# The adaptive-norm vector of a diffusion block: weight blocks as the stationary operand of TensorE, and value and key projections a quarter at a time

## The chip, the cores and the metric

The kernel runs as one program on one core of a Trainium2 chip. The metric is the device time of one execution in microseconds (us); the comparison is by the median of several executions. Engine names are those of the profile: PE is TensorE (PEld its weight loads), DVE is VectorE, ACT is ScalarE, POOL is GpSimd, SP is SyncE, which only issues DMA here.

## The reference

One transformer layer for 512 latent tokens of width 1024 with 256 context tokens. What matters here is how a conditioning vector enters: its SiLU is multiplied by a 1024 x 6144 matrix, and the six thirds of the product shift, scale and gate the layer. `mod_c` is the same for the context's vector, of which only the first two parts are used.

```python
mod_x = (silu(c) @ w_ada + b_ada)          # 1024 -> 6 x 1024
mod_c = silu(c_ctx) @ w_ada + b_ada
sh1x, sc1x, g1x, sh2x, sc2x, g2x = split(mod_x, 6)
hx = rmsnorm(x, norm1_g) * (1 + sc1x) + sh1x
hc = rmsnorm(ctx, norm1_g) * (1 + sc1c) + sh1c
q, k, v, u, ga, gp = split(hx @ w_in + b_in)       # k and v also of hc
x = x + g1x * ((sigmoid(ga) * (attn(q, k, v) @ wa) + sigmoid(gp) * (pool(u) @ wp)) @ w_out)
h2 = rmsnorm(x, norm2_g) * (1 + sc2x) + sh2x
x = x + g2x * moe(h2)                              # top 4 of 32 experts
return rmsnorm(x, final_g)
```

All is fp32. The kernel keeps that accuracy by splitting operands into a high part and a residual and adding three products (`mm3`).

## The kernel before

Activations lie channel-major: channel tile k (128 of 1024) on the partitions, tokens along the free axis. The work is written out by hand in the order in which each engine is to do it (`tc.manual_schedule`); every engine takes its instructions in that order.

**Start.** `x_load` brings the tokens, `norm1` scales them, `ht(k)` transposes channel tile k of all 768 tokens into a PSUM buffer (tag S, two of them). `wada` chunks of 1024 x 256 (1 MB) arrive in four pairs j, scale part (1) and shift part (0); each pair serves channel tiles 2j and 2j+1. `ada_mm` multiplies a chunk on TensorE with the conditioning vectors `sil` as the stationary operand (128 x 2) and the chunk as the moving one, 256 columns; the 2-row result is copied (`ada_row1`) and turned into columns by small transposes (`ada_t`). For j = 1 to 3 the scale chunk is multiplied on VectorE (latent vector) and GpSimd (context vector) instead: `gemv`, whose partial sums over the partitions come from matmuls with ones (L288). `ada_t` ends with the columns `mod` and `sca`; `h1(k)` then applies them on ScalarE and splits the result into `hx` and `hc` on VectorE. `v_part(j)` adds two channel tiles to the value projection. Of the first key tile, channel tiles 0 to 5 come before the last `v_part`; the rest of K (`k_mm`) and the first two Q tiles follow.

**Attention stage.** 16 units of 4 heads x 128 queries, each cut into six slices k. Into each slice a few matmuls of a stream (Q of later groups and the two gates, `fps`, L710) are put, by the tables `FPW` and `UW`. One more `w_ada` chunk per unit is worked on, ten in all (`ada_at`): VectorE multiplies half of its columns (`ada_mul_d`, L636 and L638, spread over the slices by `ADN`), GpSimd the other (`ada_mul_p`), and a unit later two matmuls with ones sum over the partitions (`ada_sum`, L643).

**Branch stage.** Sixteen projection tiles (L972), in whose loop the last six chunks are multiplied (`ada_mul`) and summed to rows (`ada_out`, L466). Then follow the output projection, the router, and 32 experts, whose weights stream in.

Of the kernel before, what the change touches and what calls it, by code (L numbers as in the profile page):

```python
# [43 lines left out]
R_C, R_CC, R_N1, R_PS, R_BIN, R_BADA, R_END = 0, 8, 16, 24, 32, 68, 108  # L44
# [24 lines left out]
def body(ctx, tc, x, c, cx, c_ctx, w_ada, b_ada, norm1_g, norm2_g, w_in, b_in, attn_sink, w_pool,  # L69
# [180 lines left out]
    def gemv(j):  # L250
        raw = wad.pop((j, 1))
        g = [wk.tile([P, 256], F32, tag=t, bufs=3, name="gem") for t in ("ph", "pl")]
        for k in range(KT):
            o = g[k % 2]
            if k < 2:
                dve.tensor_scalar(o, raw[:, k, :], sil[:, k, 0:1], None, op0=ALU.mult)
            else:
                dve.scalar_tensor_tensor(o, raw[:, k, :], sil[:, k, 0:1], o, op0=ALU.mult, op1=ALU.add)
        pr = [hw([P, 4, 256], F32, "gemp") for i in range(2)]
        for i in range(2):  # L260
            ks = slice(4 * i, 4 * i + 4)
            pool.tensor_mul(pr[i], raw[:, ks, :], sil[:, ks, 1:2].to_broadcast([P, 4, 256]))
        pool.tensor_add(pr[0], pr[0], pr[1])
        pool.tensor_add(pr[0][:, 0:2], pr[0][:, 0:2], pr[0][:, 2:4])
        pool.tensor_add(pr[0][:, 0], pr[0][:, 0], pr[0][:, 1])
        dve.tensor_add(g[0], g[0], g[1])
        gem[j] = (g[0], pr[0][:, 0, :])

    def ada_mm(j):
        pm = adt[j] = ps_b("PJ", "ada")  # L270
        for part in (1, 0) if j == 0 else (0,):
            raw = wad.pop((j, part))
            for k in range(KT):
# [3 lines left out]
    def ada_row1(j):  # L277
        n = L if j == 0 else 256
        mrow = wb([2, L], F32, "mrow")
        act.copy(mrow[:, 0:n], adt[j][0:2, 0:n])  # L280
        adt[j] = mrow

    def ada_t(j):
        mrow, pt, k0 = adt.pop(j), hts[2 * j], 2 * j
        for q in range(4):
            if j and q > 1:
                for v in range(2):
                    pe.matmul(pt[:, 768 + 2 * q + v:769 + 2 * q + v], gem[j][v][:, (q - 2) * P:(q - 1) * P],  # L288
                              onesf[:, 0:1], start=True, stop=True)
            else:  # L290
                pe.transpose(pt[:, 768 + 2 * q:770 + 2 * q], mrow[:, q * P:(q + 1) * P], ident[0:2, 0:2])
        for part in (1, 0):
            r = part * KT + k0
            dve.tensor_add(mod[:, r:r + 2, :],
                           pt[:, 768 + 4 * part:772 + 4 * part].rearrange("p (m s) -> p m s", s=2),
                           col[:, R_BADA + r:R_BADA + r + 2, None].to_broadcast([P, 2, 2]))
# [3 lines left out]

    gem = {}
    adt = {}
# [38 lines left out]

    with tc.manual_schedule():
        x_load(0)
        vec = wb([R_END, P], F32, "vec")
        for r, ap in ((R_C, c[0]), (R_CC, c_ctx), (R_BADA, b_ada[0, 0:5120]), (R_N1, norm1_g[0]),
# [13 lines left out]
        nc.sync.dma_start(rope, rope_t)  # L359
        norm1(0)  # L360
# [9 lines left out]
        ht(0)  # L370
        ht(1)
        for i in range(4):
            k = slice(2 * i, 2 * i + 2)
            split(wvh[:, k], wvl[:, k], wvr[:, k])
        ada_mm(0)
        ada_row1(0)
        gemv(1)
        for j in range(4):
# [70 lines left out]
    def ada_mul(raw):  # L449
# [6 lines left out]
        for k in range(1, KT):  # L456
            dve.scalar_tensor_tensor(a0, raw[:, k, 0:P], sil[:, k, 0:1], a0, op0=ALU.mult, op1=ALU.add)
            if k % 2:
                yield
# [1289 lines left out]
```

## Time and profile before

| | us |
|---|---|
| median of 3 executions (1839.09 to 1844.54) | 1843.96 |
| profiled execution, its own time | 1846.71 |
| its span, first to last instruction | 1844.9 |
| TensorE busy | 1730.0 |
| VectorE busy | 1616.3 |
| ScalarE busy | 1121.6 |
| GpSimd busy | 442.6 |

The mean granted TensorE clock of the profiled execution is 0.968 of full speed (2.4 GHz); where it is throttled it stands at 0.50 (1.2 GHz). In the rows, times are from the span's start; "PE L1020 MATMUL lcps<-wr,acol 128*128 128x32" is a matmul at line 1020 with a stationary block of 128 x 128 and a moving one of 128 rows and 32 columns. An fp32 matmul shows as two records, an fp32r one as one.

### The profile page before, as it was taken

What the parts mean: (1) busy time and instruction counts of PE and PEld (TensorE: products, weight loads), DVE (VectorE), ACT (ScalarE), POOL (GpSimd) and SP (SyncE); (2) the same over time, 40 slices, a digit from 0 to 9 for tenths busy, and PEclk for the clock granted to TensorE, in tenths of its full rate; (3) what the DMA queues carried; (4) which work ended last, traced back from release to release, by engine and by line L of the source; (5) the groups of instructions that cost most, each with busy time, mean ns of one, the idle gap of its engine ahead of it and who ended that gap; (6) DMA issues with size and microseconds to landing.
All of it is one profiled execution on the core that took longest, in us unless ns stands there. A gap on an engine that the chain in (4) does not pass through costs nothing. (4 is left out here: it accounts for less than half of the span.)

```text
span 1844.9 us, 22641 instructions
## 1 busy us (share of the span) xinstructions
PE 1730.0 (94%) x8380; PEld 1281.8 (69%) x8380; DVE 1616.3 (88%) x1687; ACT 1121.6 (61%) x1194; POOL 442.6 (24%) x275
## 2 busy tenths in 40 slices
PE   4997989999999989999999999999999999999994
PEld 2676767777778857777666777777777777777763
DVE  6469998866786689998999999999999999999994
ACT  3155656763333256777576777667777777776762
POOL 5035453412341011415241211111121121112001
PEclk8799999999999989999999999999999999999997
DMA  9031422233575599999899999999999999999972
GB/s 329 3 115 52 132 80 81 98 110 110 183 237 181 192 305 323 368 369 378 314 376 357 367 366 372 367 360 374 377 364 366 378 363 367 379 362 365 376 278 100
DMA packets 180238, 506.00 MB, mean 274 GB/s; under 512 B 12491, under 2 KB 68952, under 8 KB 180124
## 3 DMA queue, kind: packets, MB, share of 16 engines
q1 hardware_dynamic: 172028, 484.04, 72.2%
q0 software_dynamic: 8096, 20.48, 4.3%
q8 instruction: 67, 1.10, 0.2%
q14 instruction: 47, 0.39, 0.1%
HBM read 489.89 MB, written 22.69 MB: 278 GB/s over the span
## 5 line engine op out<-in xcount | busy, mean ns | idle before, releaser
L1553 DVE TENSOR_TENSOR mwl<-mw,mwh 128x2048 fp32r<-128x2048 f32 x384 | 873.2, 2283 | 37.7 <-PE gu L1283 28.0
L1546 ACT CAST mwh<-mw 128x2048 fp32r<-128x2048 f32 x384 | 727.1, 1910 | 256.2 <-PE dn L1283 116.6
L1283 PE MATMUL gu<-mwh,xT 128*96 128x512 f32 x2048 | 522.2, 397 | 3.0 <-DVE xT L125 2.7
L1283 PEld LDWEIGHTS gu<-mwh,xT 128*96 128x96 f32 x2048 | 326.5, 162 | 139.6 <-DVE xT L125 3.1
L1288 POOL DMA_INDIRECT acc<-y,igs x31 | 119.2, 3845 | 912.8 <-DVE y L1396 912.8
L1283 PE MATMUL gu<-mwl,xT 128*96 128x512 f32 x1024 | 280.5, 396 | 3.0 <-DVE mwl L1553 3.0
L1283 PE MATMUL dn<-mwh,aT 128*96 128x512 f32 x992 | 253.1, 397 | 0.0
L1283 PEld LDWEIGHTS gu<-mwl,xT 128*96 128x96 f32 x1024 | 165.9, 162 | 76.1 <-DVE mwl L1553 3.5
L1283 PEld LDWEIGHTS dn<-mwh,aT 128*96 128x96 f32 x992 | 155.4, 162 | 61.3
L1283 PE MATMUL dn<-mwl,aT 128*96 128x512 f32 x496 | 134.8, 393 | 0.0
L710 PE MATMUL fps<-hx,whi 128*128 128x512 f32 x352 | 122.8, 407 | 1.8 <-ACT rope_t L594 0.8
L1283 PEld LDWEIGHTS dn<-mwl,aT 128*96 128x96 f32 x496 | 79.9, 161 | 34.7
L1244 POOL DMA_INDIRECT xgb<-h2d,igs x31 | 87.0, 2805 | 39.7 <-DVE ltok L1178 16.9
L1373 ACT ACTIVATE gs<-gs 96x1024 f32<-96x1024 f32 x32 | 34.0, 1062 | 90.2 <-DVE gs L1370 90.2
L710 PEld LDWEIGHTS fps<-hx,whi 128*128 128x128 f32 x352 | 66.9, 191 | 18.0 <-ACT gzt L583 2.3
L710 PE MATMUL fps<-hx,wlo 128*128 128x512 f32 x176 | 70.8, 402 | 2.0 <-POOL wlo L695 2.0
L514 ACT ACTIVATE prob<-S,nm 128x512 f32<-128x512 f32 (+1 forms) x64 | 47.8, 747 | 35.4 <-DVE nm L510 34.7
L521 PE MATMUL tp<-ident,prob 128*128 128x128 f32 x288 | 45.6, 282 | 14.5 <-DVE pl L529 14.5
L529 DVE TENSOR_TENSOR pl<-tp,ph 128x512 fp32r<-128x512 f32 x72 | 49.2, 684 | 9.5 <-ACT ph L525 9.0
L509 DVE TENSOR_REDUCE nm<-S 128x1 f32<-128x512 f32 (+1 forms) x64 | 47.9, 749 | 6.4 <-PE S L484 6.0
L1396 DVE SCALAR_TENSOR_TENSOR y<-dn,gts,g2r 96x512 f32<-96x512 f32 x64 | 44.9, 740 | 4.9 <-PE dn L1283 4.9
L525 ACT CAST ph<-tp 128x512 fp32r<-128x512 f32 x72 | 42.0, 584 | 5.2 <-PE tp L521 4.6
(405 smaller groups left out, 2587.7 us busy)
## 6 DMA issues: line engine op xcount, KB each, us to landing
mw<-in_w_gu_dram SPq DMA_DIRECT2D x256, 1024.0 KB
mw<-in_w_down_dram SPq DMA_DIRECT2D x128, 1024.0 KB
wada<-in_w_ada_dram SPq DMA_DIRECT2D x24, 1024.0 KB
gz<-gzt SPq DMA_DIRECT2D x16, 256.0 KB
sg<-gz SPq DMA_DIRECT2D x16, 256.0 KB
wo<-in_w_out_dram SPq DMA_DIRECT2D x4, 1024.0 KB
xt<-in_x_dram SPq DMA_DIRECT2D x2, 1024.0 KB
xh<-in_x_dram SPq DMA_DIRECT2D x4, 512.0 KB
```

What stands on the lines that cost most here:

```text
L509: dve.reduce_max(nmh, S[:, 0:W], axis=AX.X)
L514: act.activation(U["prob"][:, h, 0:W], S[:, 0:W], AF.Exp, bias=nmh, scale=SCALE, accum_out=U["den"][:, h:h + 1])
L521: pe.transpose(U["tp", j][:, h * P:(h + 1) * P], U["prob"][:, h, j * P:(j + 1) * P], ident)
L525: act.copy(U["ph", j], U["tp", j])
L529: dve.tensor_sub(pl, U["tp", j], U["ph", j].bitcast(F32))
L710: pe.matmul(pt, a[:, k, :], b(k), start=n == 0, stop=n == 3 * KT - 1)
L1244: pool.indirect_dma_start(out=xg, out_offset=None, in_=h2d, in_offset=bass.IndirectOffsetOnAxis(ap=ig, axis=0), bounds_check=L - 1, oob_is ...
L1283: pe.matmul(os_[j], lhs(a, k), b[:, k, j * L:(j + 1) * L], start=first and j not in seen, stop=last and j not in left)
L1288: pool.indirect_dma_start(out=acc, out_offset=bass.IndirectOffsetOnAxis(ap=iscat, axis=0), in_=y, in_offset=None, bounds_check=L - 1, oob_ ...
L1396: dve.scalar_tensor_tensor(st["y"][:, cs], st["dn"][n], st["gt"], g2r[0:CAP, cs], op0=ALU.mult, op1=ALU.mult)
L1546: act.copy(hi, raw)
L1553: eng.tensor_sub(lo, raw, hi.bitcast(F32))
```

## The change

All of `w_ada` is now multiplied on TensorE, with 128 x 128 blocks of the chunk as the stationary operand and `sil` as the moving one: two columns in the start, one later. The result is a column per channel at once, so that the row copies, the transposes, `gemv`, `ada_mul`, `ada_mul_p`, `ada_mul_d` and `ada_out` are gone, as is the table `ADN`. In the attention stage thirteen chunks are done instead of ten, one at the end of each unit 0 to 12; three are left to the branch stage. The start goes quarter by quarter: transposes, the quarter's two chunks, `h1`, the quarter of V; the first key tile now gets channel tiles 0 to 3, 4 and 5, and 6 and 7 behind the second, third and fourth quarter, in an S buffer of PSUM, so that from the third quarter on only one of those is left for transposes.

```diff
+    def ada_cols(o, raw, v):
+        for m in range(2):
+            for k in range(KT):
+                pe.matmul(o(m), raw[:, k, m * P:(m + 1) * P], v(k), start=k == 0, stop=k == KT - 1)
     def ada_mm(j):
-        pm = adt[j] = ps_b("PJ", "ada")
-        for part in (1, 0) if j == 0 else (0,):
-            raw = wad.pop((j, part))
-            for k in range(KT):
-                pe.matmul(pm[0:2, part * 256:part * 256 + 256], sil[:, k, :], raw[:, k, :], start=k == 0,
-                          stop=k == KT - 1)
...
+        pm = ps_b("PJ", "ada")[:, 0:8].rearrange("p (a m s) -> p a m s", a=2, m=2)
+        for part in (1, 0):
+            ada_cols(lambda m: pm[:, part, m], wad.pop((j, part)), lambda k: sil[:, k, :])
...
+    def k_part(m, ks):
+        wh, wl = kw[m]
+        if m not in kps:
+            kps[m] = ps_s("kps")
+        for o, h0, h1 in ((kps[m][:, 0:L], hxa(0), hxa(1)),
+                          (kps[m][:, L:L + LC], lambda k: hc[0][:, k, :], lambda k: hc[1][:, k, :])):
+            for k in ks:
+                pe.matmul(o, wh(k), h0(k), start=k == 0, stop=False)
+                pe.matmul(o, wl(k), h0(k), start=False, stop=False)
+                pe.matmul(o, wh(k), h1(k), start=False, stop=k == KT - 1)
...
         wada_load(1)
+        wkr = load_w(w_in[:, OK:OK + 256], "wk_")
         wada_load(2)
-        wkr = load_w(w_in[:, OK:OK + 256], "wk_")
         wada_load(3)
...
+            ht(2 * j)
             if j < 2:
-                gemv(j + 2)
+                ht(2 * j + 1)
+            ada_mm(j)
+            h1(2 * j)
+            if j >= 2:
+                ht(2 * j + 1)
+            h1(2 * j + 1)
+            if j == 0:
+                for i in range(4):
+                    k = slice(2 * i, 2 * i + 2)
+                    split(wvh[:, k], wvl[:, k], wvr[:, k])
+            v_part(j)
+            if j == 1:
+                kw[0] = halves(wkr, 0)
+                k_part(0, range(4))
             if j == 2:
-                kw0 = halves(wkr, 0)
-            if j == 3:
-                kx = ps_b("PJ", "kps")
-                mm3(kx, *kw0, hxa(0), hxa(1), 6, last=False)
-            v_part(j)
-        kw = [kw0, halves(wkr, 1)]
+                k_part(0, range(4, 6))
+                kw[1] = halves(wkr, 1)
         for t in range(NT + NTC):
             v_out(t)
+        k_part(0, range(6, 8))
...
     def ada_sum(raw):
         pt = ps_b("PT", "adaps")
-        for m in range(2):
-            pe.matmul(pt[:, m:m + 1], raw[:, 0, m * P:(m + 1) * P], onesf[:, 0:1], start=True, stop=True)
+        ada_cols(lambda m: pt[:, m:m + 1], raw, lambda k: sil[:, k, 0:1])
         return pt
...
-    NADA = 10
-    ada_at = {u: u for u in range(8)}
-    ada_at[9], ada_at[11] = 8, 9
+    NADA = 13
...
-                q = ada_at.get(u - 1)
-                if k == 5 and q is not None:
-                    aps = ada_sum(araw[q])
+                q = u if k == 5 and u < NADA else None
+                if q is not None:
+                    aps = ada_sum(araw.pop(q))
...
-            if i % 2 == 0:
-                for _ in ada_mul(adas[q]):
-                    pass
-            else:
-                ada_out(q, adas.pop(q))
-                if q + 2 < 16:
-                    adas[q + 2] = ada_load(q + 2, 2 + q % 2)
+        if i % 2 and q < 16:
+            ada_col(q, ada_sum(adas.pop(q)))
+            if q + 2 < 16:
+                adas[q + 2] = ada_load(q + 2, 2 + q % 2)
+            if q == 15:
+                ada_row_out(12, 16)
```

How the order moves, at three places. TensorE in the start, from the first transposes to the first value matmuls (`hT` is the transposed input, `ada` the vector's PSUM tile, `vps` the value accumulator). Before:

```order
L307 MATMUL hT<-ident,xt_107 128x128 x2
L274 MATMUL ada<-wada,sil 2x256 x16
L291 MATMUL hT<-ident,mrow 128x2 x4
L274 MATMUL ada<-wada,sil 2x256 x8
L307 MATMUL hT<-ident,xt_105 128x128 x2
```

and with the change:

```order
L271 MATMUL hT<-ident,xt_107 128x128 x2
L253 MATMUL ada<-sil,wada 128x2 x32
L292 MATMUL vps<-bv,onesf 128x256
L296 MATMUL vps<-wvh,hx_77 128x256
L297 MATMUL vps<-wvh,hx_79 128x256
```

The second pair's matmuls and the next transposes no longer stand between the first pair and the value part: 32 matmuls of two columns, then directly V, which needs `hx`.

VectorE in the same place (`gem` is the partial product of `gemv`, `wvl` the residual of the value weights). Before:

```order
L125 TENSOR_TENSOR wvl<-wv__128,wvh 128x512 x4
L256 TENSOR_SCALAR gem<-wada,sil 128x256 x2
L258 SCALAR_TENSOR_TENSOR gem<-wada,sil,gem 128x256 x6
L266 TENSOR_TENSOR gem<-gem 128x256
L294 TENSOR_TENSOR mod<-hT,col 128x4 x2
L297 SCALAR_TENSOR_TENSOR sca<-mod,col 128x4
L313 CAST hx_77<-th 128x512
```

and with the change:

```order
L262 TENSOR_TENSOR mod<-ada,col 128x4 x2
L264 SCALAR_TENSOR_TENSOR sca<-mod,col 128x4
L277 CAST hx_77<-th 128x512
L278 TENSOR_TENSOR hx_79<-th,hx_77 128x512
L281 CAST hc_81<-tcx 128x256
L282 TENSOR_TENSOR hc_82<-tcx,hc_81 128x256
L277 CAST hx_77<-th 128x512
L278 TENSOR_TENSOR hx_79<-th,hx_77 128x512
L281 CAST hc_81<-tcx 128x256
L282 TENSOR_TENSOR hc_82<-tcx,hc_81 128x256
L125 TENSOR_TENSOR wvl<-wv__128,wvh 128x512 x4
```

`mod` comes first now, and the value weights are split behind the first quarter's `h1`.

TensorE at the end of a unit of the attention stage (`pv` is the unit's output, `fps` the stream, `adaps` the vector's columns). Before:

```order
L537 MATMUL pv<-ph,vx 128x512
L538 MATMUL pv<-pl,vx 128x512
L643 MATMUL adaps<-onesf,wada_668 128x1 x2
L710 MATMUL fps<-hx_77,whi 128x512
L710 MATMUL fps<-hx_77,wlo 128x512
```

and with the change:

```order
L478 MATMUL pv<-ph,vx 128x512
L479 MATMUL pv<-pl,vx 128x512
L253 MATMUL adaps<-sil,wada_702 128x1 x16
L635 MATMUL fps<-hx_78,whi 128x512
L635 MATMUL fps<-hx_78,wlo 128x512
```

Sixteen one-column matmuls stand where two stood; the stream follows as before.

## Rows read from the trace of the kernel before

**Rows 1.** The page, TensorE's granted clock in 40 slices, tenths of full speed.

```profile
PEclk8799999999999989999999999999999999999997
```

**Rows 2.** Busy time by stage: stretch; PE, PEld, DVE, ACT, POOL; clock, DMA share, GB/s.

```profile
32.00:72.20 40.20, 25.81 (x80) 16.92 (x81) 25.45 (x34) 4.95 (x9) 18.27 (x12) 0.53 0.35 115
...
72.20:123.60 51.40, 51.14 (x321) 43.29 (x319) 30.58 (x66) 21.19 (x38) 5.39 (x3) 1.00 0.26 82
...
123.60:354.50 230.90, 198.53 (x1097) 162.36 (x1098) 210.15 (x400) 149.68 (x334) 121.01 (x95) 0.97 0.27 87
...
468.00:571.00 103.00, 97.75 (x409) 75.92 (x407) 82.31 (x108) 35.87 (x47) 43.67 (x32) 0.97 0.63 200
...
655.00:1844.90 1189.90, 1156.26 (x5283) 813.05 (x5282) 1121.50 (x760) 807.39 (x559) 210.37 (x66) 0.98 0.96 349
```

**Rows 3.** The same of two units of the attention stage: units 1 and 14.

```profile
144.10:167.00 22.90, 15.73 (x86) 12.83 (x85) 22.32 (x32) 11.40 (x26) 17.14 (x13) 0.93 0.15 47
...
368.70:382.00 13.30, 13.30 (x87) 11.68 (x86) 10.48 (x22) 10.36 (x23) 2.59 (x2) 1.00 0.30 101
```

**Rows 4.** Waits of TensorE, 123.6 to 354.5 us: total, times, longest.

```profile
PE tp L521 <- DVE pl L529: 14.5, 10, 4.3
```

**Rows 5.** Timeline (start, us, instruction): loads for one-column matmuls, half and full clock.

```profile
66.54 0.50 PEld L288 LDWEIGHTS hT<-onesf,gem 128*128 128x128 f32 x2
...
67.78 0.55 PEld L288 LDWEIGHTS hT<-onesf,gemp 128*128 128x128 f32 x2
...
90.25 0.30 PEld L288 LDWEIGHTS hT<-onesf,gem 128*128 128x128 f32 x2
...
90.92 0.30 PEld L288 LDWEIGHTS hT<-onesf,gemp 128*128 128x128 f32 x2
```

**Rows 6.** Narrow matmuls in the timeline, and the busy time of stretches about them.

```profile
571.20 1.97 PE L1020 MATMUL lcps<-wr,acol 128*128 128x32 f32 x16 [0.71 <-DMA wr<-in_w_router_dram]
...
573.90:577.30 3.40, 3.40 (x19) 3.40 (x18) 3.31 (x5) 0.62 (x1) 0.00 (x0) 0.50 1.01 353
...
640.68 3.71 PE L1198 MATMUL x<-oh,xh 128*128 128x96 f32 x16
...
640.70:644.40 3.70, 3.70 (x21) 3.68 (x21) 2.03 (x7) 0.85 (x1) 0.00 (x0) 0.50 1.01 383
```

**Rows 7.** Timeline of TensorE in the start.

```profile
18.62 1.06 PE L307 MATMUL hT<-ident,xt 128*128 128x128 f32 x4
...
42.58 2.82 PE L307 MATMUL hT<-ident,xt 128*128 128x128 f32 x12 [10.62 <-ACT tcx L316]
...
52.61 1.22 PE L328 MATMUL vps<-bv,onesf 1*128 1x256 f32 x2
...
65.90 0.41 PE L334 MATMUL vps<-wvl,hc 128*128 128x256 f32 x1
```

**Rows 8.** Timeline of VectorE in the start: weight split, `mod`, `h1`.

```profile
22.05 2.50 DVE L125 TENSOR_TENSOR wvl<-wv__128,wvh 128x512 fp32r<-128x512 f32 x4 [3.52 <-ACT wvh L120]
...
68.45 0.23 DVE L294 TENSOR_TENSOR mod<-hT,col 128x4 f32<-128x4 f32 x2 [12.60 <-PE hT L288]
...
71.92 0.69 DVE L314 TENSOR_TENSOR hx<-th,hx 128x512 fp32r<-128x512 f32 x1
...
72.85 0.42 DVE L318 TENSOR_TENSOR hc<-tcx,hc 128x256 fp32r<-128x256 f32 x1
```

**Rows 9.** Timeline of TensorE: K part of six channel tiles, then V.

```profile
91.17 0.48 PE L131 MATMUL kps<-hx,whi 128*128 128x512 f32 x1
...
95.35 0.28 PE L332 MATMUL vps<-wvh,hx 128*128 128x256 f32 x1
...
95.47 0.28 PE L333 MATMUL vps<-wvh,hx 128*128 128x256 f32 x1
```

**Rows 10.** Branch stage: a wait of TensorE, and the busy time behind it.

```profile
PE adaps L466 <- issue: 4.1, 1, 4.1
...
485.00:492.10 7.10, 6.09 (x14) 4.25 (x15) 3.77 (x6) 2.73 (x4) 0.00 (x0) 0.52 0.42 135
```

More of the change, by code (lines that the diff above doesn't have):

```diff
@@ L283, in ada_t @@
[L283 to L291, printed above, removed]
+    def ada_cols(o, raw, v):
+        for m in range(2):
+            for k in range(KT):
+                pe.matmul(o(m), raw[:, k, m * P:(m + 1) * P], v(k), start=k == 0, stop=k == KT - 1)
@@ L292, in ada_t @@
+    def ada_mm(j):
+        pm = ps_b("PJ", "ada")[:, 0:8].rearrange("p (a m s) -> p a m s", a=2, m=2)
+        for part in (1, 0):
+            ada_cols(lambda m: pm[:, part, m], wad.pop((j, part)), lambda k: sil[:, k, :])
+        k0 = 2 * j
         for part in (1, 0):
             r = part * KT + k0
-            dve.tensor_add(mod[:, r:r + 2, :],
-                           pt[:, 768 + 4 * part:772 + 4 * part].rearrange("p (m s) -> p m s", s=2),
+            dve.tensor_add(mod[:, r:r + 2, :], pm[:, part],
@@ L344, in body @@
         vec = wb([R_END, P], F32, "vec")
-        for r, ap in ((R_C, c[0]), (R_CC, c_ctx), (R_BADA, b_ada[0, 0:5120]), (R_N1, norm1_g[0]),
+        for r, ap in ((R_C, c[0]), (R_CC, c_ctx), (R_BADA, b_ada[0]), (R_N1, norm1_g[0]),
                       (R_PS, pool_scale[0]), (R_BIN, b_in[0])):
@@ L447, in ada_load @@
         return raw
-    def ada_mul(raw):
-        r1 = raw[:, :, P:]
-        pool.tensor_mul(r1, r1, sil[:, :, 0:1].to_broadcast([P, KT, P]))
-        for h in (4, 2, 1):
-            pool.tensor_add(r1[:, 0:h, :], r1[:, 0:h, :], r1[:, h:2 * h, :])
-        a0 = raw[:, 0, 0:P]
-        dve.tensor_scalar(a0, a0, sil[:, 0, 0:1], None, op0=ALU.mult)
[L456 to L459, printed above, removed]
-    def ada_out(q, raw):
-        part, cc = divmod(q, 4)
-        o = wb([1, 256], F32, "adab")
-        nc.sync.dma_start(o, b_ada[0:1, 2 * D + q * 256:2 * D + (q + 1) * 256])
-        pt = ps_b("PT", "adaps")
-        pe.matmul(pt[0:1, 0:256], onesf[:, 0:1], raw[:, 0, :], start=True, stop=True)
-        dve.tensor_add(o, o, pt[0:1, 0:256])
-        nc.sync.dma_start(adad[part:part + 1, cc * 256:(cc + 1) * 256], o)
     def att_scores(S, qs, g, n, h, lo_b, nl):
@@ L563, in body @@
     pool.memset(zr, 0.0)
-    acol = cp.tile([P, 24], F32, name="acol")
+    acol = cp.tile([P, 32], F32, name="acol")
     post, lazy, due, cnt = [], [], [], [0]
@@ L737, in body @@
         aps = None
[L738 to L740 removed]
+        kput0 = k_epi(0, kps[0][:, 0:L], kps[0])
+        k_part(1, range(KT))
         wq0 = halves(wqr, 0)
@@ L805, in body @@
                     due.remove(d)
-                if k == 5 and q is not None:
+                if q is not None:
                     ada_col(q, aps)
-                if k == 5 and u == 13:
-                    ada_row_out()
-                if k == 0 and q is not None:
-                    for kk in ADN[k]:
-                        ada_mul_d(araw[q], kk)
-                q = ada_at.get(u)
-                if k and q is not None:
-                    if k == 3:
-                        ada_mul_p(araw[q])
-                    for kk in ADN[k]:
-                        ada_mul_d(araw[q], kk)
+                if k == 5 and u == NADA:
+                    ada_row_out(0, 12)
                 wsum += FPW[k] * UW.get(u, 1.0)
@@ L956, in body @@
     raw, braw, sgs = None, br_load(0), br_gate(0)
-    adas = {NADA: ada_load(NADA, 2), NADA + 1: ada_load(NADA + 1, 3)}
-    for dst, part in ((g1b, 2), (t2b, 3)):
+    adas = {NADA + i: ada_load(NADA + i, 2 + (NADA + i) % 2) for i in range(2)}
+    for dst, part in ((g1b, 2), (t2b, 3), (s2b, 4)):
         nc.sync.dma_start(dst, bc_row(adad[part - 2], D))
```

90 lines of the change are left out of this document (11 added, 79 removed).

## The prediction, on record before the changed kernel was run

> **What bounds the kernel now.** I read the summary's clock line first, then the busy time by stage, then inside the stages that the change touches: the waits, the timeline, and the granted clock of short stretches.
>
> The clock line [rows 1] shows full speed nearly everywhere, with its loss in the first slices. By stages [rows 2]: the start falls into two halves. From 32.0 to 72.2 us TensorE is busy for 25.8 of 40.2 us, at a mean clock of 0.53. It waits 10.6 us for `h1`, which waits for the modulation vector [rows 7], and then works at half speed. From 72.2 to 123.6 us, where the first score matmul starts, it is busy for 51.1 of 51.4 us at full clock. The attention stage up to 354.5 us (the thirteen units 0 to 12) takes 230.9 us: TensorE is busy for 198.5, VectorE for 210.2. So it waits for VectorE in some units; the longest in sum are for the residual of the probabilities, 14.5 us [rows 4]. In a unit without modulation work, such as 368.7 to 382.0 us, TensorE has no gap at all, against 15.7 of 22.9 us in unit 1 [rows 3]. From 655 us on, nothing is changed; TensorE is busy for 1156 of 1190 us there [rows 2], and its weight loads have a fixed ring of buffers, so I let every microsecond of the first 655 pass through to the end.
>
> **The price of the new block.** The change multiplies one 1024 x 256 chunk by 16 fp32 matmuls with a 128 x 128 stationary block and one or two moving columns. The nearest rows are the sums over partitions (L288), the same stationary shape with one moving column. At half clock three of them take from 66.54 to 67.78 us, 0.413 us each; at full clock 90.25 to 90.92, 0.223 us each [rows 5]. A chunk then costs 3.6 us at full and 6.6 us at half clock; the two chunks of one step of the start, 7.1 or 13.2 us.
>
> Which of the two? Eight fp32 matmuls of 32 columns (L1020, two records each) keep TensorE busy for 2 us from 571.2 us; right behind them the clock is at 0.50 from 573.9 to 577.3 us, though the dense output projection has begun. Eight of 96 columns (L1198) keep it busy for all of 3.7 us from 640.7 us and end at 0.50 as they began [rows 6]. So being busy with narrow matmuls neither holds the clock nor brings it back, and one or two columns are narrower than any of these. I take the blocks as losing the clock. The Trainium skill ("TensorE: Matmul & The Clock Gate", section "Why this matters for your kernels") says that the clock is lost through idle gaps between bursts of matmuls; a block has no gap, and by that rule alone the sum would be that of the first rival below, 1849 us. The rows just named speak against reading it so.
>
> **The start.** Removed: three chunks' multiplications on VectorE and GpSimd (`gemv`), the row copies and transposes (`ada_row1`, `ada_t`). Added: eight chunks instead of five on TensorE, and TensorE now runs each quarter as a chain: block, `mod`, `h1`, V part. I follow it.
>
> - Block 0 starts at 19.7 us behind the first transposes, as now; four of those take 1.06 us, half clock [rows 7]. 13.2 us: 32.9.
> - `mod` to the second channel tile's last residual takes 4.2 us (68.45 to 72.61), 4.9 with the context's [rows 8]; the first split of the value weights, now behind it, 0.6 more: 38.4.
> - V part 0 runs at half clock now: five of its six token tiles take from 52.61 to 66.3 us [rows 7]. 13.7, and 1.5 for the rest of the first: 53.6.
> - Twelve transposes 2.8 [rows 7], block 1 13.2, chain 4.2: 73.8. Up to here it is level with now (75.0 us).
> - V part 1 has 36 matmuls of 0.12 us, K part 0 to 3 twelve of 0.232 (18 take from 91.17 to 95.35) and twelve of 0.12 [rows 9]: 8.5. A dense run behind a narrow one begins at half clock. The spell at 573.9 us, within dense work, lasts 3.4 us [rows 6] and so costs 1.7: 84.0.
> - Quarters 2 and 3: six transposes 0.7; a block, between 7.1 and 13.2 since the clock is up when it starts, 10.2 taken (the middle, for want of a nearer row); the chain, now 5 because the K accumulator holds one of the two PSUM buffers and the second tile's transposes come behind the first tile's `h1`; V and K part 6.4 and 1.7. Quarter 2 ends at 108.0; 123.9 for the chain of quarter 3.
> - Then dense: V 4.3, K rest 2.1, second K tile 8.5, Q 48 x 0.232 = 11.1, a spell 1.7: 151.6; first score at 152.
>
> That is **28 us later** than 123.6. Low end: blocks 2 and 3 at full clock and no spells, 11 less, +17. High end: both at half clock and their dense runs too, 15 more, +43. The queue of loads on SyncE is no bound: `wk` goes ahead of two chunks and the last chunk waits for the buffer of block 1's first half, free near 63 us, and is wanted at 114. That cover is 50 us.
>
> **The attention stage.** Ten chunks' multiplications go from VectorE and GpSimd, thirteen blocks come to TensorE. TensorE's work in units 0 to 12 now is 198.5 busy less 6.9 (lost to spells of half clock: the stage's mean is 0.97 of 230.9 us [rows 2]; in unit 1 it is 0.93 [rows 3]) less 4.5 (ten pairs of the old sums at 0.223): 187.1 at full clock. The blocks add 13 x 16 x 0.223 = 46.4. Each block is followed by dense stream matmuls, and I charge one spell of 1.7 per block: 22. Some waiting stays, above all in the first units, which are filled with rotary work; I leave 5 of the 32.4 us that TensorE idles in this stage. Sum 261 against 230.9: **30 us longer**. Low end +18 (half of the blocks without a spell), high end +40 (some with two). VectorE's load falls below TensorE's, so its lateness no longer counts. The pending `ada_col` makes VectorE wait for the block; behind it stands the next unit's maximum, which needs scores that TensorE issues after the block anyway.
>
> **The branch stage.** Removed: the wait of 4.1 us for the first product and the half clock behind it, 7.1 us at 0.52, 3.4 lost [rows 10]; six one-row sums of two pairs' time, 0.45 each, 2.7. Added: three blocks with a spell each, 15.9. **+6 us** (+1 to +10). Rows of the bias and the outputs, now two DMAs instead of seven, and the broadcast of the scale row moved ahead of the loop are not waited for: the stage's only long wait is the one named. GpSimd is far from any bound.
>
> **Sum.** 28 + 30 + 6 = 64. The profiled execution took 1846.7 us, 2.7 above the runs' median of 1844.0; on the median the forecast is 1908.
>
> **Rivals.**
> 1. The blocks keep the clock. Then block 0 ends at 26.8, V part 0 takes 7.6, and so on with full prices: first score at about 120, -4; attention 187.1 + 46.4 + 5 = 239, +8; branch +1. 1849. For it: TensorE has no gaps in a block. Against: [rows 6]. Chance 0.13.
> 2. Faster: the start gains more than the rest loses. What it would take: the half-clock stretch from 32.0 to 72.2, 14.4 us idle and 25.8 at half speed [rows 2], becomes one dense run. 14.4 and 12.9 go, the three added chunks cost 10.7, the chains hide under V and K parts: -16. With attention +3 and branch +1, 1832. It decides if the clock is up from block 0 on. In attention nothing can be gained: TensorE has 32.4 idle, 6.9 and 4.5, together 43.8 us to give back, 3.4 per block, and a block costs 3.6 even at full clock. Chance 0.05.
> 3. The clock stays low for longer than one spell behind every block, in the start as well: attention +22 more, start +43, branch +10. 1949. For it: from 640.7 the clock stays at half through all the narrow work [rows 6]. Against: the dense stream behind a block is long. Chance 0.10.
>
> The forecast has 0.72.
>
> **How the numbers follow.** A measurement can tell about 0.3% (5.5 us) from no change. Forecast and rival 3 are slower (0.82), and of rival 1, which lies near that edge, 0.04: 0.86. Within: 0.08 of rival 1. Faster: rival 2 and 0.01 of rival 1: 0.06. The sum's own ends (each stage's low or high end together) are 1844 + 36 = 1880 and 1844 + 93 = 1937. To hold 8 in 10, I go from 1868 (part of the way to rival 1) to 1945 (nearly all the way to rival 3). What is left out is rivals 1 and 2, 0.18, and little else.
>
> **What would show it.** Right: granted clock about half in every block of two-column matmuls and just behind it; first score near 152 us; 0.41 us a matmul in blocks 0 and 1; units 0 to 12 at 18 to 21 us each, without waits for VectorE; VectorE less busy than TensorE in every unit; the branch stage without its 4 us wait. Wrong: a clock of 1.0 through the blocks with first scores before 125 us; blocks much cheaper than 0.22 us a matmul; or TensorE still idle in the units for VectorE.

## The result and the profile after

The changed kernel takes 1910.9 us (median of 4 executions, 1904.6 to 1917.2), the kernel before 1842.1 beside it: 1.037 times as long, with a 95% interval of 1.033 to 1.042. The forecast was 1908, between 1868 and 1945. The profiled execution took 1904.6 us, the shortest of the four, 6.3 below the median; the stages are read from it, so they say nothing of these 6.3. The page of it, span, busy time of each engine and the clock line that answers to [rows 1]:

```profile
span 1902.6 us, 23561 instructions
PE 1821.8 (96%) x8983; PEld 1395.7 (73%) x8983; DVE 1495.7 (79%) x1532; ACT 1120.4 (59%) x1191; POOL 340.4 (18%) x196
...
PEclk9778989899999989999999999999999999999997
```

TensorE is busy for 92 us more than before, VectorE for 121 less. The clock line has lost tenths in slices 3, 4, 6 and 8: what the line showed lost only at the very start before is now lost in the attention stage too. (Its first slice has gained one; the last section says why that is no gain.) Busy time by stage, the same columns as [rows 2], but with the changed kernel's own borders (first score at 150.3 us, unit 13 at 408.2, branch from 522.1 to 629.9, experts from 715.4):

```profile
72.20:150.30 78.10, 71.82 (x396) 66.42 (x395) 25.33 (x54) 19.73 (x35) 5.39 (x3) 0.76 0.16 54
150.30:408.20 257.90, 251.44 (x1474) 219.13 (x1474) 152.35 (x323) 149.72 (x335) 74.70 (x55) 0.90 0.28 94
522.10:629.90 107.80, 107.25 (x494) 89.65 (x492) 49.59 (x56) 37.18 (x48) 9.87 (x7) 0.94 0.52 165
715.40:1902.60 1187.20, 1153.71 (x5281) 811.45 (x5280) 1121.09 (x759) 807.50 (x559) 213.31 (x66) 0.99 0.96 350
```

The two profiled spans differ by 57.7 us, the two medians by 68.9. The start has 26.7 of them (first score at 150.3 instead of 123.6), units 0 to 12 have 27.0 (257.9 instead of 230.9), the branch stage 4.7 (107.9 instead of 103.2, up to the router's first matmul). The rest is level: the stretches between, 199.4 instead of 197.5, and the experts, 1187.2 instead of 1189.7.

In the attention stage TensorE is now the bound by far: 251.4 of 257.9 us, VectorE 152.4. Its waits there, the two longest; the first of them is one wait in unit 0, and what stood in [rows 4], 14.5 us for the residual `pl`, is nearly gone. The third line is a stretch that begins within the block of unit 4 (247.2 to 251.9 us): TensorE has no gap in it, and the clock is at half.

```profile
PE S L413 <- ACT prob L455: 3.2, 1, 3.2
PE pv L479 <- DVE pl L470: 1.7, 3, 1.0
...
249.40:256.20 6.80, 6.80 (x27) 6.03 (x27) 0.90 (x3) 0.40 (x1) 0.00 (x0) 0.50 0.89 300
```

And the start on TensorE's timeline (start, duration, line): the four blocks, what stands behind the second and the third, and the first score; the last line is busy time and clock from 4 us into the third block to near the end of its V part.

```profile
19.58 13.65 PE L253 MATMUL ada<-sil,wada 128*128 128x2 f32 x64
...
53.40 2.20 PE L271 MATMUL hT<-ident,xt 128*128 128x128 f32 x12
55.43 11.05 PE L253 MATMUL ada<-sil,wada 128*128 128x2 f32 x64
68.26 0.58 PE L296 MATMUL vps<-wvh,hx 128*128 128x256 f32 x1 [1.77 <-DVE hx L277]
...
81.51 9.93 PE L253 MATMUL ada<-sil,wada 128*128 128x2 f32 x64
93.24 1.54 PE L271 MATMUL hT<-ident,xt 128*128 128x128 f32 x6 [1.80 <-ACT tcx L280]
...
106.11 10.56 PE L253 MATMUL ada<-sil,wada 128*128 128x2 f32 x64
...
150.27 0.39 PE L413 MATMUL S<-kkc,qs 128*128 128x256 f32 x1 [1.03 <-DVE qs L401]
...
85.60:102.70 17.10, 14.40 (x65) 13.73 (x66) 4.99 (x12) 3.40 (x5) 0.00 (x0) 0.50 0.18 57
```

A block of 32 narrow matmuls takes 13.65 us where the clock is at half (0.43 each) and 10 to 11 where it is up at its beginning and falls within it. The gaps between a block and the V part behind it are short, 1.8 us and in the last two quarters 0.75 more.

### The profile page after: what moved, and what is told of

The parts are those of the page before. It is cut to its first block, busy times and chain, and to the rows that moved or that the text cites. A ratio compares the mean times of both kernels' runs of the same rounds, so it can differ in the third digit from the quotient of the medians.

```text
span 1902.6 us, 23561 instructions
## 1 busy us (share of the span) xinstructions
PE 1821.8 (96%) x8983; PEld 1395.7 (73%) x8983; DVE 1495.7 (79%) x1532; ACT 1120.4 (59%) x1191; POOL 340.4 (18%) x196
## 5 line engine op out<-in xcount | busy, mean ns | idle before, releaser
L635 PE MATMUL fps<-hx,whi 128*128 128x512 f32 x352 | 130.9, 432 | 1.4 <-ACT rope_t L535 0.8
L635 PEld LDWEIGHTS fps<-hx,whi 128*128 128x128 f32 x352 | 71.4, 205 | 17.9 <-ACT gzt L524 1.7
L253 PEld LDWEIGHTS adaps<-sil,wada 128*128 128x128 f32 x512 | 64.7, 205 | 1.2
L253 PE MATMUL adaps<-sil,wada 128*128 128x1 f32 x512 | 63.1, 257 | 0.0
L276 ACT ACTIVATE th<-hT,mod,sca 128x512 f32<-128x512 f32 x8 | 6.2, 777 | 94.0 <-DVE sca L264 61.8
```

The costliest lines, as they stand in the source:

```text
L253: pe.matmul(o(m), raw[:, k, m * P:(m + 1) * P], v(k), start=k == 0, stop=k == KT - 1)
L276: act.activation(th, pt[:, 0:L], AF.Identity, bias=mod[:, k, 0:1], scale=sca[:, k, 0:1])
L635: pe.matmul(pt, a[:, k, :], b(k), start=n == 0, stop=n == 3 * KT - 1)
```

## The experiments

**Theory.** A block of narrow matmuls costs TensorE its own time and, besides, the clock: dense work behind it runs at half for a while. **Rivals.** Only TensorE's own work counts, and the clock is an accident of the stage. Or, in the start: the serial order of the quarters costs, not the clock. "Lost to half clock" below is a stretch times one less its mean clock; the clock stands in the rows with two digits, so for the attention stage such a figure is good to some 1.3 us.

**1. The chunk as the moving operand, in nine of thirteen units and in the branch.**

```diff
         pt = ps_b("PT", "adaps")
-        ada_cols(lambda m: pt[:, m:m + 1], raw, lambda k: sil[:, k, 0:1])
+        if q in range(4, 8):
+            ada_cols(lambda m: pt[:, m:m + 1], raw, lambda k: sil[:, k, 0:1])
+            return pt
+        for k in range(KT):
+            pe.matmul(pt[0:1, 0:256], sil[:, k, 0:1], raw[:, k, :], start=k == 0, stop=k == KT - 1)
```

> The changed kernel, but in nine of the units 0 to 12 (0 to 3, 8 to 12) and in the branch stage a chunk is multiplied by eight matmuls with the vector as stationary operand (128 x 1) and 256 moving columns, 0.44 us each at full clock (16 records from 80.7 to 84.0 us in the trace of before), so the same 3.5 us of TensorE as a block of sixteen narrow ones. Units 4 to 7 keep the narrow blocks. Theory (narrow moving operands lose the clock): units 0 to 12 lost 26 us to half clock in the changed kernel and 7 before; 9/13 of the difference comes back, 13 us, and some 3 in the branch: 1895 us, the stage from first score to unit 13 at 245 instead of 258, half-clock spells mainly in units 4 to 7. Rival (only TensorE's own work counts): no change, 1908 to 1914. Rival (a product with one column or one row of the array leaves the clock down whatever moves): no change, with the same spells.

Measured: 1884.7 us, 1.022 of before (1.019 to 1.025). Busy time: the attention stage; 3.4 us behind the narrow block of unit 4; a wide block in unit 11 and what follows it; the branch stage.

```profile
153.50:399.20 245.70, 238.47 (x1330) 184.96 (x1330) 156.23 (x323) 149.21 (x335) 74.76 (x55) 0.97 0.29 98
249.00:252.40 3.40, 3.40 (x14) 2.81 (x12) 0.42 (x1) 0.41 (x1) 0.00 (x0) 0.50 1.08 378
375.70:382.50 6.80, 6.80 (x34) 3.96 (x33) 2.44 (x5) 3.71 (x7) 2.54 (x2) 1.00 0.55 182
512.30:613.40 101.10, 101.10 (x447) 77.94 (x445) 50.45 (x56) 36.81 (x47) 9.87 (x7) 1.00 0.54 173
```

The stage is at 245.7, as the theory had it. Behind the narrow blocks of units 4 to 6 the clock falls to 0.50 (not behind that of unit 7), behind no wide block does it, and the branch stage keeps full clock throughout: 101.1 us, 6.8 less than with three narrow blocks. Same chunk, same 3.5 us of TensorE, one vector column, but the operands have changed places: eight matmuls with 256 moving columns and a narrow stationary operand stand for sixteen with one moving column, each with a 128 x 128 weight load of its own. That speaks against both rivals; which of these counts, the moving width or the weight loads, no run here separates, and "narrow" below stands for both. The total is 10 us under the 1895 expected: the branch gave some 4 of them, and the rest was not traced to a stage.

**2. The narrow matmuls spread over the unit.** The sixteen go by fours into slices 0 to 3, one behind each stream matmul, into unused columns of the slice's score buffer.

```diff
+    def ada_part(raw, i, S):
+        return [partial(pe.matmul, S[:, 768 + m:769 + m], raw[:, k, m * P:(m + 1) * P], sil[:, k, 0:1],
+                        start=k == 2 * i, stop=k == 2 * i + 1) for m in range(2) for k in (2 * i, 2 * i + 1)]
...
+                    if todo:
+                        todo.pop(0)()
```

> The changed kernel, but the sixteen one-column matmuls of a unit go four each into slices 0 to 3, one behind each stream matmul, instead of in one block in slice 5; their sums are added up by three more small VectorE additions a unit. TensorE's work is the same. Theory (a block of 3.6 us of narrow work loses the clock, a narrow matmul among wide ones does not): 15 to 20 us less, 1891 to 1896, stage of units 0 to 12 at 238 to 243 us, its mean clock at 0.97 as before. Rival (only the work counts): no change, 258 us, 1908 to 1914. Rival (the added VectorE steps and waits in every slice cost what the clock gives back): clock 0.97 but 250 us or more.

Measured: 1909.0 us (1.034 to 1.037 of before); the stage took 267.7 us. The stage, the two longest waits of TensorE in it, and the longest of the first kind, in unit 0, with the instruction that it waits for:

```profile
150.20:417.90 267.70, 245.17 (x1473) 209.97 (x1474) 155.12 (x362) 151.31 (x334) 74.63 (x55) 0.94 0.26 87
```

```profile
PE S L751 <- DVE nm L450: 16.9, 16, 6.6
PE S L751 <- DMA wada<-in_w_ada_dram: 3.0, 2, 2.8
...
157.76 0.68 DVE L450 TENSOR_REDUCE nm<-S 128x1 f32<-128x512 f32 x1
158.49 0.58 PE L751 MATMUL S<-sil,wada 128*128 128x1 f32 x2 [6.60 <-DVE nm L450]
```

A miss, and a confounded one: the clock came up (0.94 instead of 0.90), but TensorE waited 16.9 us until VectorE had read the maximum from the same score buffer, though it reads other columns of it. The Trainium skill ("PSUM — Partial Sum Buffer", section "PSUM bank collisions raise a hardware error") says to guard PSUM by bank, not by address. The wait here does not go by the columns read either: in unit 0 the maximum reads 512 columns, and the matmuls into columns 768 and 769 waited for it all the same, 8.3 of the 16.9 us. In this kernel the buffer as a whole is guarded; whether less would do was not tried. So the place was badly chosen, and the next run moves it.

**3. The same, ahead of the scores.**

```diff
+                    if u < NADA:
+                        for f in ada_part(araw[u], k, A["S", k]):
+                            f()
                     att_scores(A["S", k], qs_[g], A["g"], A["n"], k, A["lo"], A["nl"])
```

> As the run with the matmuls spread over four slices, but each slice's four one-column matmuls stand ahead of the slice's score matmuls in the same PSUM buffer, so that TensorE no longer waits for the maximum over that buffer (16.9 us in that run, and 3.0 for chunks just loaded). TensorE's work is that of the changed kernel. Theory (a block of sixteen loses the clock, four at a time do not): stage of units 0 to 12 at 238 to 245 us instead of 257.9, with at most 10 us lost to half clock, 1890 to 1898. Rival (only the work counts, and waits found their way back in as soon as the clock was up): 255 to 262 us, 1908 to 1914.

Measured: 1882.2 us (1.018 to 1.023). The stage:

```profile
151.00:395.20 244.20, 234.77 (x1466) 205.87 (x1467) 153.52 (x362) 150.63 (x334) 74.51 (x55) 0.96 0.29 95
```

257.9 became 244.2 with every narrow matmul still there, and the loss to half clock 9.8 instead of 25.8 us. Four narrow matmuls at a time do not lose the clock that sixteen in a row lose: two half-clock spells are left in the stage, 10.2 us each, and both stand beside a wait of TensorE, 2.4 us in unit 0 and 4.8 us, up to 338.8 us, for a chunk still on its way. The total is some 8 us under the range expected, which the stage does not explain.

**4. How much a block costs.** Two one-column matmuls for each chunk instead of sixteen, in the attention and branch stages.

```diff
-        ada_cols(lambda m: pt[:, m:m + 1], raw, lambda k: sil[:, k, 0:1])
+        for m in range(2):
+            pe.matmul(pt[:, m:m + 1], raw[:, 0, m * P:(m + 1) * P], onesf[:, 0:1], start=True, stop=True)
```

> The changed kernel with two one-column matmuls per chunk instead of sixteen in the attention and branch stages: the products over seven eighths of the conditioning vector are left out there, the chunks are still loaded and the small additions stay. Only the stages up to the branch are to be read. What a block costs: fourteen matmuls at 0.223 are 3.1 us, 41 for the thirteen. Theory (each block loses the clock as well): units 0 to 12 at 193 to 200 us instead of 257.9, thus 4.5 to 5 us a block, with under 6 us lost to half clock. Rival (only the work counts): 217 us. Rival (the work is hidden behind waits anyway): 230 or more.

Measured, in one execution, the attention and the branch stage:

```profile
147.20:347.40 200.20, 190.83 (x1110) 160.35 (x1111) 154.29 (x323) 148.79 (x334) 75.42 (x55) 0.99 0.35 116
460.50:552.00 91.50, 91.50 (x410) 75.48 (x408) 49.63 (x56) 35.90 (x47) 9.88 (x7) 1.00 0.59 190
```

(257.9 - 200.2) / 13 = 4.4 us for fourteen matmuls, whose own time is 3.1; in the branch (107.9 - 91.5) / 3 = 5.5. That is more than the work alone, by which the stage should have stood at 217 us, and at the edge of the theory's 4.5 to 5 in attention. The stage without blocks also shows about what can be won there: 200 us against 230.9 before the change.

**5. The start with the chunk as the moving operand, same order.**

```diff
+            for k in range(KT):
+                pe.matmul(pm[0:2, part * 256:part * 256 + 256], sil[:, k, :], raw[:, k, :], start=k == 0,
+                          stop=k == KT - 1)
+        mrow = wb([2, L], F32, "mrow")
+        act.copy(mrow, pm[0:2, :])
+        for q in range(4):
+            pe.transpose(pt[:, 768 + 2 * q:770 + 2 * q], mrow[:, q * P:(q + 1) * P], ident[0:2, 0:2])
```

> The changed kernel with its order of quarters, but each chunk of the start is the moving operand again (256 columns), and its two-row result is copied and turned by four small transposes. TensorE's work is within 1 us; each chain gets a copy and transposes longer, about 2 us. Theory (the narrow blocks hold the clock down: half from 58.3 to 75.4, 85.6 to 102.7 and 109.5 to 126.6 us): blocks 2 and 3 and the dense work behind them run at full clock, some 8 us back for each, 2 lost in each of four chains: first score at 140 to 144 us instead of 150, 1901 to 1905. Rival (the serial order of the quarters is what costs, not the clock): first score at 155 to 160, 1916 to 1921.

Measured: 1896.4 us (1.028 to 1.031), first score at 137.4. Three of its blocks on the timeline, and busy time with the granted clock behind the second and the third:

```profile
19.57 7.51 PE L260 MATMUL ada<-wada,sil 128*2 128x256 f32 x32
...
74.49 7.07 PE L260 MATMUL ada<-wada,sil 128*2 128x256 f32 x32
...
96.33 7.07 PE L260 MATMUL ada<-wada,sil 128*2 128x256 f32 x32
```

```profile
61.50:68.30 6.80, 6.12 (x25) 5.53 (x26) 3.70 (x8) 1.61 (x3) 0.00 (x0) 0.50 0.26 91
85.40:92.20 6.80, 5.81 (x26) 5.23 (x26) 3.31 (x6) 2.17 (x3) 0.00 (x0) 0.50 0.24 78
```

Each block now takes 7.1 us, at full clock, the very first included, instead of 13.7, 11.1, 9.9 and 10.6. So 12.9 us come back, somewhat more than the theory had asked for. But a second loss shows: behind each block there is the wait for `mod` and `h1`, in gaps of 0.7 and 1.8 us with four two-column transposes between them, and the V part that follows it begins at half clock. Here the loss stands beside idle gaps, of which the Trainium skill's rule in the prediction ("TensorE: Matmul & The Clock Gate", section "Why this matters for your kernels") speaks, though the gaps that it names are longer than these; the narrow blocks lose the clock without one.

**6. The next quarter's chunks ahead of the V part.** Wide chunks as in 5, so that TensorE works while `h1` is computed; and the same order with the narrow blocks.

```diff
+        ada_mm(0)
         for j in range(4):
-            ht(2 * j)
+            ada_t(j)
...
+            if j < 3:
+                ada_mm(j + 1)
             v_part(j)
...
+            if j < 3:
+                ht(2 * j + 2)
+                if j < 1:
+                    ht(2 * j + 3)
```

> The changed kernel with the chunks of the start as moving operands, and with the next quarter's two chunks multiplied ahead of the present quarter's V part, so that TensorE works while h1 is computed. Theory (of the 26.7 us that the start lost, 13 were the clock and went with the wide form; of the other 14, 10.5 are the three chunks that TensorE has more, and the rest the chain of each quarter): with the chain covered the first score comes at 120 to 128 us instead of 137.4, 1879 to 1887. Rival (the start then waits for chunks instead, which are wanted a quarter sooner): first score at 132 or later, 1891 or more.

> The changed kernel with its narrow blocks in the start, but each quarter's block ahead of the former quarter's V part, as in the run with wide chunks ahead; the four of them make a square of order and width: 150.3 us (serial, narrow), 137.4 (serial, wide), 114.5 (ahead, wide) to the first score. Theory (the narrow blocks run at half clock and hold it down, whatever the order): blocks 0 to 2 at 13.2 instead of some 7 to 8 and dense runs behind them at half: 130 to 138 us, 1885 to 1895. Rival (the serial order was all of it): 114 to 118, 1868 to 1873.

Wide and ahead: 1868.3 us (1.012 to 1.016), first score at 114.5, 9 us earlier than in the kernel before. Narrow and ahead: 1903.4 us (1.027 to 1.034), first score at 144.6. Blocks on the timeline, wide (its last line is a stretch with its clock), then narrow, with V matmuls of the narrow run:

```profile
19.71 8.68 PE L262 MATMUL ada<-wada,sil 128*2 128x256 f32 x32
...
29.39 7.07 PE L262 MATMUL ada<-wada,sil 128*2 128x256 f32 x32
...
47.18 7.07 PE L262 MATMUL ada<-wada,sil 128*2 128x256 f32 x32
...
114.53 0.39 PE L431 MATMUL S<-kkc,qs 128*128 128x256 f32 x1 [1.04 <-DVE qs L419]
...
23.00:84.50 61.50, 56.96 (x332) 35.95 (x330) 18.34 (x46) 15.20 (x25) 0.00 (x0) 1.00 0.40 141
```

```profile
19.65 13.65 PE L253 MATMUL ada<-sil,wada 128*128 128x2 f32 x64
...
33.67 13.78 PE L253 MATMUL ada<-sil,wada 128*128 128x2 f32 x64 [0.37 <-PE ada L253]
...
66.17 13.65 PE L253 MATMUL ada<-sil,wada 128*128 128x2 f32 x64
...
80.04 0.41 PE L302 MATMUL vps<-wvh,hx 128*128 128x256 f32 x1
80.25 0.41 PE L303 MATMUL vps<-wvl,hx 128*128 128x256 f32 x1
...
85.54 0.28 PE L302 MATMUL vps<-wvh,hc 128*128 128x256 f32 x1
85.66 0.28 PE L303 MATMUL vps<-wvl,hc 128*128 128x256 f32 x1
```

In the narrow run V matmuls stand 0.21 us apart until 85 us and 0.12 right after: with narrow blocks ahead of every V part, TensorE does not leave half clock for the first 85 us, though it has no gap from 33.7 us on (51.5 of 51.5 us busy). First score in the four cases: serial narrow 150.3, serial wide 137.4, ahead narrow 144.6, ahead wide 114.5. The order alone brings 6, the width alone 13, both 36. (The serial narrow start stands in five of the kernels, with first scores from 147.2 to 153.5, so the 6 are close to what such a reading can tell.) Neither theory had this: I expected 120 to 128 for the wide and 130 to 138 for the narrow run, as if the two added up. They need each other, since either loss keeps the clock down for the other: cover without wide blocks is dense work at half, wide blocks without cover have gaps behind them.

**7. The old start under the new attention stage.** The start of the kernel before, with `gemv`, row copies and its order:

```diff
+        ada_mm(0)
+        ada_row1(0)
+        gemv(1)
         for j in range(4):
-            ht(2 * j)
...
-            ada_mm(j)
+            ada_t(j)
+            if j < 3:
+                ada_mm(j + 1)
```

> The start of the kernel before (gemv on VectorE and GpSimd, wide chunks on TensorE, its order), and the attention and branch stages of the changed one. If the stages add up: 26.7 us less than the changed kernel, 1884, first score at 124, units 0 to 12 at 258 us. If the attention stage only looks slow because the start hands it late data or a low clock: units 0 to 12 nearer 240, 1866.

Measured: 1877.6 us (1.017 to 1.020), first score at 123.1. The stage:

```profile
123.10:386.60 263.50, 255.56 (x1474) 222.31 (x1474) 153.61 (x323) 149.47 (x335) 74.57 (x55) 0.89 0.27 91
```

The 27 us of the start come back whole, so the attention stage does not owe its time to the start. It even takes 5.6 more than in the changed kernel: the code is the same, but 29 us are lost to half clock instead of 25.8. The median, 1877.6, is below the 1884 expected; against the profiled execution of the changed kernel, the shortest of its four, its span is 26 us less (1876.6 against 1902.6).

**8. What would have been faster.** If units 0 to 12 wait for VectorE before the change, VectorE has to be relieved without a burden on TensorE. Three versions on the kernel before, and a last one that joins what won. All chunks of the attention stage on GpSimd, both halves (`k in (1, 3)`), and six wide chunks in the branch:

```diff
-    def ada_mul_p(raw):
-        r1 = raw[:, :, P:]
+    def ada_mul_p(raw, m):
+        r1 = raw[:, :, m * P:(m + 1) * P]
...
-                    if k == 3:
-                        ada_mul_p(araw[q])
-                    for kk in ADN[k]:
-                        ada_mul_d(araw[q], kk)
+                    if k in (1, 3):
+                        ada_mul_p(araw[q], k // 2)
```

> The kernel before, but both halves of a chunk in the attention stage are multiplied on GpSimd (VectorE's 48.5 us of such work there go, GpSimd's go from 46 to some 92 of 121 to 167), and in the branch stage the six chunks are moving operands of eight 256-column matmuls instead of products on VectorE and GpSimd. Theory (in the kernel before, units 0 to 12 wait for VectorE, and what is taken from VectorE without being put on TensorE is gained): TensorE has 192 us at full clock there, with 5 to 10 idle and 3 to 7 lost to half clock 200 to 208 us instead of 230.9, and the branch 101 instead of 103: 1812 to 1820. Rival (GpSimd then delivers the residuals of the stream's weights late, or slows VectorE): stage at 225 or more, 1838 or more.

Or half of each chunk as eight narrow matmuls on TensorE, the other half on GpSimd, with the same branch:

```diff
+        for k in range(KT):
+            pe.matmul(pt[:, 0:1], raw[:, k, 0:P], sil[:, k, 0:1], start=k == 0, stop=k == KT - 1)
+        pe.matmul(pt[:, 1:2], raw[:, 0, P:2 * P], onesf[:, 0:1], start=True, stop=True)
```

> The kernel before, but VectorE's half of each of the ten chunks in the attention stage goes to TensorE as eight one-column matmuls, in the place of the old sums, GpSimd keeps its half, and the branch stage has the wide matmuls. Half a block is 1.8 us of narrow work. Theory by the sum: 192 us of TensorE, 17.8 for the half blocks, 5 idle, and spells behind some of them, up to 10 times 1.7: 215 to 232 us; if half a block is too short to lose the clock 215 to 220, so 1826 to 1833. Rival (every narrow burst costs a spell, however short): 230, 1841.

Measured: 1839.5 us for the first (0.997 to 1.000 of before) and 1851.4 for the second (1.003 to 1.006), both some 20 more than expected. Attention and branch of the first, then attention of the second:

```profile
123.30:335.40 212.10, 191.75 (x1097) 159.83 (x1098) 179.86 (x320) 149.63 (x334) 166.94 (x135) 0.98 0.29 95
449.70:565.10 115.40, 113.06 (x494) 81.12 (x492) 51.25 (x58) 35.24 (x45) 10.97 (x9) 1.00 0.56 180
```

```profile
123.40:348.10 224.70, 209.60 (x1238) 178.38 (x1239) 168.61 (x320) 149.85 (x335) 120.93 (x95) 0.97 0.28 90
```

The attention stage gained 18.8 with GpSimd and 6.2 with half blocks; both kept a clock of 0.97 to 0.98, so eight narrow matmuls in a row are hardly punished either: behind two of the ten half blocks the clock fell. What I had wrong is the branch: I took 101 us for it from experiment 1, where it has three chunks; here it has six. 91.5 without chunks and six times 3.5 are 113, measured 115.4, and that ate most of the gain.

Then the first version with the branch stage of before, each chunk's sum one projection tile later:

```diff
+        if i % 2 == 0:
+            if NADA <= q - 1 < 16:
+                ada_out(q - 1, adas.pop(q - 1))
```

> The kernel before with two edits and no block on TensorE at all: in the attention stage both halves of a chunk on GpSimd (as in the run before, where that stage took 212.1 instead of 230.9 us), and in the branch stage the old products on VectorE and GpSimd with each chunk's sum one projection tile later, so that TensorE no longer waits 4.1 us for the first one and keeps its clock. Expected: attention 212, branch 95 to 98 instead of 103.2 (4.1 of wait and 3.4 of half clock go): 1816 to 1821. Rival (the branch's wait only moves to the next tile, since GpSimd waits for the chunk's load): branch 103, 1824.

Measured: 1830.8 us, 0.993 of before (0.992 to 0.994). Attention 214.1; the branch 104.5, no shorter, since its wait only moved:

```profile
PE brps L131 <- DVE wlo L125: 5.7, 5, 2.4
```

That is VectorE, late with the residual of the next projection's weights; the chunk's products stand ahead of them. So the last version puts these on GpSimd as well, the sums three tiles later, and takes the start of experiment 6:

```diff
+    def ada_mul(raw):
+        for m in range(2):
+            r1 = raw[:, :, m * P:(m + 1) * P]
+            pool.tensor_mul(r1, r1, sil[:, :, 0:1].to_broadcast([P, KT, P]))
+            for h in (4, 2, 1):
+                pool.tensor_add(r1[:, 0:h, :], r1[:, 0:h, :], r1[:, h:2 * h, :])
...
+        if i % 2 and NADA <= q - 1 < 16:
+            ada_out(q - 1, adas.pop(q - 1))
```

> The parts that won, together: the start of the run with wide chunks a quarter ahead (first score at 114.5 us instead of 123.6), the attention stage of before with both halves of a chunk on GpSimd (214.1 and 212.1 us instead of 230.9), and a branch stage with the six chunks wholly on GpSimd and their sums three projection tiles later, so that neither VectorE (the 5.7 us of waits for wlo in the run before) nor the first product (4.1 us) is waited for: 94 to 97 us instead of 103.2. Expected if the stages add up: 1843 - 9 - 18 - 7 = 1809, 1805 to 1814. Rival (GpSimd, with more than 60 of 95 us of work in the branch, is late and the wait goes there): branch 103, 1817.

Measured: **1813.4 us, 0.984 of before (0.983 to 0.986)**: faster than both kernels. First score at 113.9; attention and branch:

```profile
113.90:324.40 210.50, 193.09 (x1097) 160.97 (x1098) 179.03 (x320) 149.19 (x334) 166.91 (x135) 0.98 0.29 96
437.40:538.50 101.10, 96.65 (x410) 75.37 (x409) 60.20 (x58) 36.78 (x47) 77.25 (x55) 0.98 0.64 207
```

The start and the attention stage gave what they had given apart; the branch gave 2 us instead of 6 to 9, with 4.4 us of waits for weight splits left: 2.6 for VectorE's, where 5.7 stood, and 1.8 for ScalarE's. Without the products on VectorE about half of that wait went.

## Why the prediction was right

The mechanism was right, and the terms were near; that 1908 and 1910.9 lie so close is in part luck. The stages as traced add up to 58 us where 64 were forecast, and the other 11 of the 69 us between the medians belong to no stage: the traced execution of the changed kernel is 6.3 below its median, that of the kernel before 4.7 above.

**The price of the block** was right, and so was what it rested on: being busy with narrow matmuls does not hold the clock [rows 6]. The work was put at 3.6 us a block; 4.4 and 5.5 us for fourteen of the sixteen matmuls (experiment 4) leave the rest to the clock. The charge of one spell, 1.7 us a block, came out as 25.8 / 13 = 2.0, with one spell of 1.7 counted in that no block makes (160.7 to 164.1 us, beside the 3.2 us wait in unit 0). Behind ten of the thirteen blocks the clock is at half, behind three it is not. Rival 1, that blocks keep the clock because TensorE has no gap in them, falls with experiments 1 and 3: the clock returns with the width or the spreading, with no gap closed.

**The start**, forecast 28 later, was 26.7, but three of its steps were off and nearly cancel. The chain behind blocks 1 to 3, put at 4.2 to 5 us, left TensorE idle for only 2.0 to 2.6: the V part begins 1.8 us after block 1, because its first matmul needs only the first channel tile's `hx`, where I had waited for the second's. And block 1 took 11.05 instead of 13.2, the clock being up at its beginning. The chains came out 7 us shorter in all, the blocks 2. Against that V parts 1 to 3 ran at half clock for 6.9, 8.2 and 6.9 us, most of each, so that 11 us were lost where three spells of 1.7 had been charged. Quarter 1 ended at 80.9 instead of 84.0, block 3 began at 106.1 instead of 108.7, the first score came at 150.3 instead of 152.

**The attention stage**, forecast 30 longer, was 27.0. Waits 6.5 for 5, clock 25.8 for 22; the dense work of 187 was some 4 too high, since without blocks TensorE is busy for 190.8 us at 0.99 with 26 one-column matmuls in it (5.8 us), which leaves 183. The picture of equal units of 18 to 21 us was wrong: they took 16.7 to 27.0, unit 0 the longest (20.5 before), with two half-clock spells and a 3.2 us wait in it. That VectorE's lateness stops counting was right, 14.5 us of waits for `pl` became 1.7.

**The branch**, forecast 6 longer, was 4.7; the 4.1 us wait is gone, and three blocks cost 5.5 each instead of 5.3.

**Rival 2** named the condition under which the start gains: the clock up from block 0 on and the chain hidden. Experiment 6 makes both true, and the start is 9 us shorter than before; the change itself makes neither true. That attention can't gain by blocks on TensorE was right for whole chunks: even spread or wide, thirteen of them leave the stage at 244 to 246, above 230.9. For halves it was not, since ten half blocks, with the other halves on GpSimd, left it at 224.7 (experiment 8). Rival 3, more than one spell behind every block, did not come: four of the thirteen have a spell of some 7 us instead of 3.4.

## What to carry to other kernels

To multiply a matrix by one vector on TensorE, let the matrix move and the vector stand: here that took the same 3.5 us a chunk, but the clock stayed up, and dense work beside it ran at full speed where TensorE had no gaps. Where columns are wanted and the matrix has to stand, cut the narrow matmuls into groups of four between wide ones, in a PSUM buffer that no other engine has still to read. And before work is moved off an engine that is waited for, ask which engine has the slack: here it was GpSimd, not TensorE, which was 86% busy in that stage already.

## What I had not expected of the hardware

- The first work decides whether the clock comes up: 16 matmuls with 256 moving columns from 19.6 us take 7.5 to 8.7 us in the eight kernels that have them, 32 with two columns from the same point 13.65 in all six others, and in the run with narrow blocks ahead V matmuls are at half spacing until 85 us. The moving width alone does not explain that: in this run V part 0, all of it matmuls with 256 moving columns, goes on without a gap from 47.4 to 63.6 us and stays at half spacing, 0.21 us.
- In the clock column a stretch ahead of the first clock record reads 1.00, whatever the matmuls do: the first slice of the clock line shows 9, where block 0 runs at half spacing. In the start the spacing of matmuls has to be read beside it.
- The same attention code, thirteen blocks in the same places, lost 25.8, 29, 32 and 38 us to half clock in four kernels that differ in the start alone (257.9, 263.5, 264.0 and 270.2 us). The wide start of experiment 6, a fifth, took 260.2. The longest is experiment 6 with narrow blocks:

```profile
144.60:414.80 270.20, 262.75 (x1474) 228.64 (x1475) 153.91 (x323) 149.48 (x335) 74.55 (x55) 0.86 0.27 90
```

What decides between them was not tried. It need not be the start: each figure is from one execution, and the four executions of the changed kernel alone spread over 12.6 us. Either way it moves the total by up to 12 us, so the terms of such a sum can't be held to less.
